# An S5 mixer on one core: states-to-outputs operand left compact, two products summed by TensorE

## The chip, the cores and the metric

The kernel runs on one core of a Trainium2 chip. The metric is the device time of one execution in microseconds (us). TensorE (PE in the profile; PEld is its weight load), VectorE (DVE), ScalarE (ACT), GpSimd (POOL) and SyncE (SP, which issues the transfers) each run a fixed order of instructions and wait for each other by semaphores.

## The reference

A trunk of two layers over 512 positions of 1024 features: an S5 state-space mixer, a shared key and value, a differential attention, a gated convolution MLP after each. Only the mixer is touched. Its core, with 64 groups of 16 channels and 64 complex states each:

```python
u = h @ w_in
def chunk_step(carry, u_chunk):
    x_r0, x_i0 = carry
    bu_r = jnp.einsum("tbgc,gpc->tbgp", u_chunk, bb_r)
    bu_i = jnp.einsum("tbgc,gpc->tbgp", u_chunk, bb_i)
    pw_r, pw_i, s_r, s_i = lax.associative_scan(_ssm_combine, (a_r, a_i, bu_r, bu_i), axis=0)
    x_r = s_r + pw_r * x_r0 - pw_i * x_i0
    x_i = s_i + pw_r * x_i0 + pw_i * x_r0
    y = (jnp.einsum("tbgp,gcp->tbgc", x_r, cr)
         - jnp.einsum("tbgp,gcp->tbgc", x_i, ci))
    return (x_r[-1], x_i[-1]), y
y = y + d_skip.astype(f32) * u.astype(f32)
g = jax.nn.gelu(y).astype(h.dtype)
val, gate = jnp.split(g @ w_glu, 2, axis=-1)
return val * jax.nn.sigmoid(gate)
```

## The kernel before

`ssm()` runs from about 26 to 168 us of the span. It treats the 64 groups in 8 blocks of 8 groups, as four pairs q of two groups g: the 128 partitions of a state tile hold the 64 states of both groups of a pair. Time is folded: four neighbouring positions make one of 128 columns, so that the positions inside a fold need a small Toeplitz product of their own.

For one block b the steps are, in the program's order:

- `cprod` (L479 to L494, VectorE): the compact tile `wo`, both operands of the block without the zeros; `ssm_coefs` loads its input `bc`.
- `ssm_prep` (L505): `pad` (L500, ScalarE) spreads `wo` into `wp` (states' inputs) and `op` (outputs). Each holds both groups of a pair side by side, zero where partition and column belong to different groups; a mask as the scale makes the zeros. `op` takes two calls of 128x512 for the four powers and two of 128x128 for slot 0, from `bc`. Then `wp` is turned (L522) and copied to `ctrl` (L523).
- `ssm_turn_u` (L552, L554): the inputs turned, `uc`. `ssm_toep` (L532): the Toeplitz operand from `wp` and `op`; it leaves PSUM by a ScalarE copy (L541) and a VectorE add of the skip term `dm` (L542), and is repeated down the partitions by three copies (L544).
- `ssm_inputs` (L563): the inputs of the states, `v`, to PSUM.
- `ssm_states` (VectorE): rotation by the tables `tab` (L582 into `za`, L583 into `zb`, added at L584), a scan for each of real and imaginary part (L586, from `za` into `zb`), rotation back: two products (L587 into `xs`, L588 into `za`) and their sum (L589, `xs` += `za`).
- `ssm_out`: `y` in one PSUM bank, for each pair q a Toeplitz product (L598) and two products with the states (L600, real and imaginary, all 128 partitions); then the gelu (L602). `ssm_turn`: `g` turned (L611, `gt`), split in a high and a low part (`hTh` L615 on ScalarE, `hTl` L616 on VectorE); `gv` is the product with `w_glu` that follows (L119 to L121, three passes: high by high, low by high, high by low), whose weights L103 (ScalarE) and L104 (VectorE) split as they come from HBM.

The loop `for b in range(-2, 11)` overlaps blocks: one turn holds `ssm_prep` and the inputs of block b+1, states and outputs of block b, the turn of b-1, the `gv` step of b-3 and the tables (`ssm_tables`, L460 to L474, with a GpSimd copy of `decay`, L467) of b+2. A scheduler fixes from it the order of each engine. The products of the second half of `u` (L119 to L121) fill in between. Two things tie the steps beside the data. The tag `tp` has two PSUM banks, shared in turn by `ct`, `ut`, `toep`, `gt` and `y`. The tags "xn" (`za`, `zb`) and "gain" (`xs`) have two buffers of 128x1024 each, so that a block's `za` and `zb` take the two of the block before.

Of the kernel before, what the change touches and what calls it, by code (L numbers as in the profile page):

```python
# [18 lines left out]
P = 128  # L19
# [33 lines left out]
class Trunk:  # L53
# [244 lines left out]
    def ssm_load(self, sp):  # L298
        nc, io = self.nc, self.io
        xk = io["x"].rearrange("t p d -> (t p) d").rearrange("(k j) d -> k j d", j=4)  # L300
        par = sp.tile([P, 158], F32, name="s5", bufs=1)
# [175 lines left out]
    def cprod(self, sp, m, b):  # L477


        V = self.nc.vector  # L480
        sh = [P, 8, 4, 16]
        wo = sp.tile([P, 2, 2, 4, 4, 16], F32, tag="wo", name=f"wo{b}", bufs=1)
        o = wo.rearrange("p r s q n c -> p r (s q) n c")
        t = sp.tile(sh, F32, tag="wot", name=f"wot{b}", bufs=1)
        k = [self.co[:, r, b].rearrange("p s q (n o) -> p (s q) n o", o=1).broadcast_to(sh) for r in range(2)]
        mr = [m[:, r].rearrange("p s q (o c) -> p (s q) o c", o=1).broadcast_to(sh) for r in range(2)]
        V.tensor_tensor(o[:, 0], k[0], mr[0], ALU.mult)
        V.tensor_tensor(t, k[1], mr[1], ALU.mult)
        V.tensor_tensor(o[:, 0], o[:, 0], t, ALU.subtract)
        t = sp.tile(sh, F32, tag="wot", name=f"wot2_{b}", bufs=1)  # L490
        V.tensor_tensor(o[:, 1], k[0], mr[1], ALU.mult)
        V.tensor_tensor(t, k[1], mr[0], ALU.mult)
        V.scalar_tensor_tensor(o[:, 1, :4], o[:, 1, :4], -1.0, t[:, :4], ALU.mult, ALU.subtract)
        V.tensor_tensor(o[:, 1, 4:], o[:, 1, 4:], t[:, 4:], ALU.add)  # L494
        return wo
    def pad(self, dst, src):

        for g in range(2):
            d = dst[:, :, :, g, :].rearrange("p (r q) n c -> p r q n c", r=2)
            self.nc.scalar.activation(d, src, AF.Copy, scale=self.maskS[:, g:g + 1])  # L500

    def ssm_coefs(self, sp, b):
        bc = sp.tile([P, 2, 2, 4, 16], F32, tag="bc", name=f"bc{b}", bufs=2)
        self.nc.sync.dma_start(bc, self.io["s5_bc"][b])
        return bc, self.cprod(sp, bc, b)  # L505

    def ssm_prep(self, sp, b, coefs):

        nc = self.nc
        bc, wo = coefs  # L510
        wp = sp.tile([P, 8, 4, 2, 16], F32, tag="wp", name=f"wp{b}", bufs=1)
        self.pad(wp, wo[:, :, 0])
        op = sp.tile([P, 8, 5, 2, 16], F32, tag="op", name=f"op{b}", bufs=2)
        self.pad(op[:, :, 1:], wo[:, :, 1])
        self.pad(op[:, :, 0:1], bc[:, :, 1].rearrange("p r q (o c) -> p r q o c", o=1))
        op = op.rearrange("p (r q) n g c -> p r q (n g c)", r=2)
        wp = wp.rearrange("p (r q) n g c -> p r q (n g c)", r=2)
# [6 lines left out]
        return ctrl, wp, op  # L524

    def ssm_toep(self, sp, b, wp, op):

        nc = self.nc
        ps = self.bank(f"toep{b}", "tp")
        for q in range(4):  # L530
            for r in range(2):
                nc.tensor.matmul(ps[:32, q * P:(q + 1) * P], wp[:, r, q, 0:32], op[:, r, q, 0:128],  # L532
                                 start=(r == 0), stop=(r == 1))
        toep = self.toep[b % 2]
        tv = toep.rearrange("p (q n) -> p q n", q=4)
        pv = ps.rearrange("p (q n) -> p q n", q=4)
        dm = sp.tile([32, 4, 32], F32, tag="dm", name=f"dm{b}", bufs=1)
        nc.gpsimd.tensor_tensor(dm, self.ident[:32, :32].rearrange("p (o c) -> p o c", o=1).broadcast_to([32, 4, 32]),
                                self.dskip[:32, 4 * b:4 * b + 4].rearrange("p (q o) -> p q o", o=1).broadcast_to([32, 4, 32]),
                                ALU.mult)  # L540
        nc.scalar.copy(tv[96:, :, 32:], pv[:32, :, 32:])  # L541
        nc.vector.tensor_tensor(tv[96:, :, :32], pv[:32, :, :32], dm, ALU.add)  # L542
        for j in range(1, 4):
            nc.scalar.copy(tv[96 - 32 * j:P - 32 * j, :, 32 * j:], tv[96:, :, :P - 32 * j])  # L544
        return toep

    def ssm_turn_u(self, sp, b, U):
# [18 lines left out]
    def ssm_states(self, sp, b, v, tab):  # L566

        nc, V = self.nc, self.nc.vector
        tab, dk = tab
        za = self.npool.tile([P, 2, 512], F32, tag="xn", name=f"za{b}")  # L570
        zb = self.npool.tile([P, 2, 512], F32, tag="xn", name=f"zb{b}")
        xs = self.npool.tile([P, 2, 512], F32, tag="gain", name=f"xs{b}")
        k4 = lambda z: z.rearrange("p r (q k) -> p r q k", q=4)
        new = lambda z: k4(z)[:, :, :, 1:]
        sh = [P, 2, 4, P - 1]
        both = lambda z, k: z.rearrange("p (r q k) -> p r q k", r=1, q=4)[:, :, :, k].broadcast_to(sh)

# [12 lines left out]
        return xs  # L590

    def ssm_out(self, sp, b, op, toep, uc, xs):
# [8 lines left out]
        g = sp.tile([P, 4, 4, 32], F32, tag="g", name=f"g{b}", bufs=2)  # L601
        nc.scalar.activation(g.rearrange("p i q e -> p q i e"), y.rearrange("p (q i e) -> p q i e", q=4, i=4),  # L602
                             AF.Gelu_apprx_tanh)
        return g
# [468 lines left out]
def pack(inp):  # L1073
# [21 lines left out]
    st = lambda n: a[n][0].reshape(32, 2, 64).transpose(1, 2, 0).reshape(P, 32)  # L1095
    grid = np.tile(np.concatenate([16 * np.arange(4), np.arange(16) + 0.5]).astype(np.float32), (P, 1))
    mask = (np.arange(P)[:, None] // 64 == np.arange(2)[None]).astype(np.float32)
    dsk = np.tile(a["ssm_d"][0].reshape(32, 32).T, (4, 1))
    cols = lambda g: g.reshape(KD, P).T
    dt = np.repeat(a["ssm_log_dt"][0].reshape(32, 2).T, 64, axis=0)  # L1100
    o["s5"] = np.concatenate([cols(a["ssm_norm"]), mask, dsk, st("ssm_lambda_re"), st("ssm_lambda_im"), grid, dt], 1)
# [45 lines left out]
```

## Time and profile before

| | us |
|---|---|
| median of 3 runs | 1348.28 |
| lowest, highest | 1346.69, 1348.58 |
| the profiled execution | 1347.01 |
| its span | 1345.2 |
| PE busy | 1313.6 (98%) |
| PEld busy | 1079.9 (80%) |
| DVE busy | 783.6 (58%) |
| ACT busy | 615.0 (46%) |
| POOL busy | 93.2 (7%) |

The span runs from the first to the last instruction of the profiled execution; its own time is 1.8 us longer. Busy shares are averages over stages with different limits, so the mixer is read by itself. The granted TensorE clock is given as a share of full speed (1.00 is 2.4 GHz, 0.50 is 1.2 GHz).

### The profile page before, as it was taken

What the parts mean: (1) busy time and instruction counts of PE and PEld (TensorE: products, weight loads), DVE (VectorE), ACT (ScalarE), POOL (GpSimd) and SP (SyncE); (2) the same over time, 40 slices, a digit from 0 to 9 for tenths busy, and PEclk for the clock granted to TensorE, in tenths of its full rate; (3) what the DMA queues carried; (4) which work ended last, traced back from release to release, by engine and by line L of the source; (5) the groups of instructions that cost most, each with busy time, mean ns of one, the idle gap of its engine ahead of it and who ended that gap; (6) DMA issues with size and microseconds to landing.
All of it is one profiled execution on the core that took longest, in us unless ns stands there. A gap on an engine that the chain in (4) does not pass through costs nothing.

```text
span 1345.2 us, 16605 instructions
## 1 busy us (share of the span) xinstructions
PE 1313.6 (98%) x6444; PEld 1079.9 (80%) x6444; DVE 783.6 (58%) x1314; ACT 615.0 (46%) x1049; POOL 93.2 (7%) x101
## 2 busy tenths in 40 slices
PE   7999799999999999999999999999999999999998
PEld 5787688988788888888887777688888888888887
DVE  8999834666633566444545665745766435664343
ACT  7899433544421344233535565644544323443242
POOL 2135000000000000000030121000000000000000
PEclk9999999999999999999999999999999999999999
DMA  6301422333333233323333102122333333333311
GB/s 219 106 25 44 134 94 63 106 104 95 95 96 101 85 95 104 102 79 106 114 111 125 62 2 73 53 69 75 125 94 94 110 95 91 99 101 100 95 56 39
DMA packets 37099, 122.31 MB, mean 91 GB/s; under 512 B 4339, under 2 KB 6387, under 8 KB 37020
## 3 DMA queue, kind: packets, MB, share of 16 engines
q1 hardware_dynamic: 35804, 119.07, 28.2%
q10 hardware_dynamic: 1184, 2.16, 0.4%
q8 instruction: 51, 0.84, 0.3%
q14 instruction: 28, 0.23, 0.1%
q0 software_dynamic: 32, 0.02, 0.0%
HBM read 119.12 MB, written 2.12 MB: 90 GB/s over the span
## 4 chain that ended last, share of the span: by engine, by line
PE 84%; DVE 11%; ACT 3%; issue 1%; DMA 0%; POOL 0%; SPq 0%; ACTq 0%; DVEq 0%
PE up L120 12%; PE up L119 12%; PE up L121 12%; PE dn L119 6%; PE dn L121 6%; PE dn L120 6%; PE pg L121 2%; PE pg L119 2%; PE pg L120 2%; PE s L957 2%; DVE zb L586 1%; PE o L979 1%; PE k L119 1%; PE q L119 1%; PE q L121 1%
## 5 line engine op out<-in xcount | busy, mean ns | idle before, releaser
L104 DVE TENSOR_TENSOR lo_wst<-wst,hi_wst 128x1024 fp32r<-128x1024 f32 x162 | 198.0, 1223 | 262.5 <-ACT hi_wst L103 262.0
L120 PE MATMUL up<-hTl,hi_wst 128*128 128x512 f32 (+1 forms) x768 | 285.6, 372 | 0.3 <-DVE hTl L167 0.3
L119 PE MATMUL up<-hTh,hi_wst 128*128 128x512 f32 (+1 forms) x768 | 285.1, 372 | 0.8 <-ACT hTh L166 0.7
L121 PE MATMUL up<-hTh,lo_wst 128*128 128x512 f32 (+1 forms) x768 | 285.1, 371 | 0.0
L103 ACT CAST hi_wst<-wst 128x1024 fp32r<-128x1024 f32 x162 | 169.8, 1049 | 231.5 <-PE dn L121 143.0
L119 PEld LDWEIGHTS up<-hTh,hi_wst 128*128 128x128 f32 x768 | 144.4, 188 | 26.8 <-ACT hTh L166 1.6
L120 PEld LDWEIGHTS up<-hTl,hi_wst 128*128 128x128 f32 x768 | 144.6, 188 | 25.6 <-DVE hTl L167 0.7
L121 PEld LDWEIGHTS up<-hTh,lo_wst 128*128 128x128 f32 x768 | 144.6, 188 | 24.9
L119 PE MATMUL dn<-hi_wst,ih 128*128 128x512 f32 x352 | 137.6, 391 | 0.0
L120 PE MATMUL dn<-lo_wst,ih 128*128 128x512 f32 x352 | 137.0, 389 | 0.0
L121 PE MATMUL dn<-hi_wst,il 128*128 128x512 f32 x352 | 136.4, 389 | 0.0
L243 DVE SCALAR_TENSOR_TENSOR acc<-up,cw,acc 128x511 f32<-128x511 f32 x88 | 65.7, 746 | 47.1 <-ACT acc L242 47.1
L242 ACT ACTIVATE acc<-up,cw 128x512 f32<-128x512 f32 x88 | 68.4, 777 | 47.3 <-PE up L121 47.3
L250 ACT CAST ih<-acc 128x512 fp32r<-128x512 f32 x44 | 27.3, 621 | 113.1 <-DVE acc L247 113.0
L119 PEld LDWEIGHTS dn<-hi_wst,ih 128*128 128x128 f32 x352 | 66.1, 188 | 14.5 <-issue 1.0
L109 DVE SCALAR_TENSOR_TENSOR lo_wst<-wst,gains,hi_wst 128x512 fp32r<-128x512 f32 x80 | 56.1, 746 | 37.0 <-ACT hi_wst L108 37.0
L121 PEld LDWEIGHTS dn<-hi_wst,il 128*128 128x128 f32 x352 | 66.1, 188 | 13.6
L120 PEld LDWEIGHTS dn<-lo_wst,ih 128*128 128x128 f32 x352 | 66.1, 188 | 13.5
L244 DVE SCALAR_TENSOR_TENSOR acc<-up,cw,acc 128x510 f32<-128x510 f32 x88 | 65.8, 748 | 2.9
L108 ACT ACTIVATE hi_wst<-wst,gains 128x512 fp32r<-128x512 f32 x80 | 53.4, 719 | 27.9 <-PE dn L121 16.9
L246 ACT ACTIVATE acc<-acc 128x512 f32<-128x512 f32 x44 | 27.8, 632 | 64.8 <-DVE acc L244 64.8
L121 PE MATMUL pg<-hi_wst,hTl 128*128 128x512 f32 (+1 forms) x128 | 49.2, 384 | 0.0
(267 smaller groups left out, 2221.7 us busy)
## 6 DMA issues: line engine op xcount, KB each, us to landing
wst<-in_w_up SPq DMA_DIRECT2D x88, 512.0 KB, 3.5
wst<-in_w_down SPq DMA_DIRECT2D x44, 512.0 KB, 3.6
wst<-in_w_glu SPq DMA_DIRECT2D x16, 512.0 KB, 3.6
wst<-in_w_gate SPq DMA_DIRECT2D x16, 512.0 KB, 3.6
wst<-in_kv_w SPq DMA_DIRECT2D x16, 512.0 KB, 4.5
wst<-in_w_in SPq DMA_DIRECT2D x8, 512.0 KB, 6.5
wst<-in_w_q SPq DMA_DIRECT2D x8, 512.0 KB, 4.7
wst<-in_w_o SPq DMA_DIRECT2D x8, 512.0 KB, 4.4
```

The source lines that it names most:

```text
L103: nc.scalar.copy(hi, st)
L104: nc.vector.tensor_tensor(lo, st, hi.bitcast(F32), ALU.subtract)
L108: nc.scalar.activation(hi[:, c], st[:, c], AF.Copy, scale=g[:, k:k + 1])
L109: nc.vector.scalar_tensor_tensor(lo[:, c], st[:, c], g[:, k:k + 1], hi[:, c].bitcast(F32), ALU.mult, ALU.subtract)
L119: nc.tensor.matmul(out, ah, bh, start=start, stop=False)
L120: nc.tensor.matmul(out, ah, bl, start=False, stop=False)
L121: nc.tensor.matmul(out, al, bh, start=False, stop=stop)
L242: nc.scalar.activation(c, ps[s], AF.Identity, bias=self.cw[:, n, 3:4], scale=self.cw[:, n, 2:3])
L243: nc.vector.scalar_tensor_tensor(c[:, 1:], ps[s][:, :T - 1], self.cw[:, n, 1:2], c[:, 1:], ALU.mult, ALU.add)
L244: nc.vector.scalar_tensor_tensor(c[:, 2:], ps[s][:, :T - 2], self.cw[:, n, 0:1], c[:, 2:], ALU.mult, ALU.add)
L246: nc.scalar.activation(acc[0], acc[0], AF.Gelu_apprx_tanh)
L250: nc.scalar.copy(ih, acc[1])
```

## The change

It does four things. (1) L589 goes: `xs` and `za` are both handed to TensorE, which multiplies each by the same operand and sums in PSUM. (2) `op` with its four ScalarE calls goes. The operand is `wo` itself, with a fifth slot, filled by a GpSimd copy (L496). Since it holds no zeros, each group's 64 states are multiplied alone, on half of TensorE's rows, into a PSUM bank of its own: 32 products of 64 rows and 64 columns a block instead of 8 of 128 by 128. The Toeplitz part of `y` becomes 8 products of 64 columns instead of 4 of 128. (3) The Toeplitz products (now L526) give 64 columns each instead of 128, and leave PSUM by two masked ScalarE calls (L535), with VectorE's add (L537) in SBUF behind them. (4) The gelu (L605) is two calls of 128x256. The other steps have new line numbers: `za`, `zb` and their sum L577, L578, L579; scan L581; back L582, L583; Toeplitz part and states part of `y` L594, L601; `v` L558; `gt` L614, `hTh` L618, `hTl` L619.

```diff
     def cprod(self, sp, m, b):
-        wo = sp.tile([P, 2, 2, 4, 4, 16], F32, tag="wo", name=f"wo{b}", bufs=1)
-        o = wo.rearrange("p r s q n c -> p r (s q) n c")
+        wo = sp.tile([P, 2, 2, 4, 5, 16], F32, tag="wo", name=f"wo{b}", bufs=3)
+        o = wo.rearrange("p r s q n c -> p r (s q) n c")[:, :, :, 1:, :]
...
+        self.nc.gpsimd.tensor_copy(wo[:, :, 1, :, 0, :], m[:, :, 1])
         return wo
...
-        self.pad(wp, wo[:, :, 0])
-        op = sp.tile([P, 8, 5, 2, 16], F32, tag="op", name=f"op{b}", bufs=2)
-        self.pad(op[:, :, 1:], wo[:, :, 1])
-        self.pad(op[:, :, 0:1], bc[:, :, 1].rearrange("p r q (o c) -> p r q o c", o=1))
+        for g in range(2):
+            nc.scalar.activation(wp[:, :, :, :, g, :], wo[:, :, 0, :, 1:, :], AF.Copy, scale=self.maskS[:, g:g + 1])
...
         for q in range(4):
             for r in range(2):
-                nc.tensor.matmul(ps[:32, q * P:(q + 1) * P], wp[:, r, q, 0:32], op[:, r, q, 0:128],
-                                 start=(r == 0), stop=(r == 1))
+                nc.tensor.matmul(ps[:32, q * 64:(q + 1) * 64], wp[:, r, q, 0:32],
+                                 wo[:, r, 1, q, :4, :].rearrange("p n c -> p (n c)"), start=(r == 0), stop=(r == 1))
...
-        nc.scalar.copy(tv[96:, :, 32:], pv[:32, :, 32:])
-        nc.vector.tensor_tensor(tv[96:, :, :32], pv[:32, :, :32], dm, ALU.add)
+        for g in range(2):
+            nc.scalar.activation(tv[96:, :, g, :], ps[:32, :256].rearrange("p (q n) -> p q n", q=4), AF.Copy,
+                                 scale=self.mask32[:, g:g + 1])
+        nc.vector.tensor_tensor(tv[96:, :, :, :16], tv[96:, :, :, :16], dm.rearrange("p q (g c) -> p q g c", g=2), ALU.add)
...
         V.tensor_tensor(new(za), both(zb[:, 1], now), pair(0, 1), ALU.mult)
-        V.tensor_tensor(xs, xs, za, ALU.add)
-        return xs
+        return xs, za
...
-        y = self.bank(f"y{b}", "tp")
+        y = [self.bank(f"y{b}_{g}", "tp") for g in range(2)]
+        at = lambda q: (slice(q * P, (q + 1) * P), slice(q * 64, (q + 1) * 64))
         for q in range(4):
-            c = slice(q * P, (q + 1) * P)
-            nc.tensor.matmul(y[:, c], uc[:, c], toep[:, c], start=True, stop=False)
-            for r in range(2):
-                nc.tensor.matmul(y[:, c], xs[:, r, c], op[:, r, q, 32:], start=False, stop=r == 1)
...
+            c, d = at(q)
+            for g in range(2):
+                nc.tensor.matmul(y[g][:, d], uc[:, c], toep[:, q * P + 64 * g:q * P + 64 * g + 64], start=q == 0, stop=False)
+        for q in range(4):
+            c, d = at(q)
+            for z in xs:
+                for r in range(2):
+                    for g in range(2):
+                        h = slice(64 * g, 64 * g + 64)
+                        nc.tensor.matmul(y[g][:, d], z[h, r, c], wo[h, r, 1, q, 1:, :].rearrange("p n c -> p (n c)"),
+                                         start=False, stop=q == 3 and r == 1 and z is xs[-1])
```

Between block 6's last product and block 7's states, VectorE's order before (the number behind a name is the block, the last one the tile's own; `wst` is a weight of `gv` or of the MLP):

```order
L588 TENSOR_TENSOR za6_1425<-zb6_1426,tab6_1249 128x8x127 [waits DVE_49]
L104 TENSOR_TENSOR lo_wst13_1626_1629<-wst13_1626,hi_wst13_1626_1628 128x1024 [waits DMAHW5_49]
L589 TENSOR_TENSOR xs6_1427<-xs6_1427,za6_1425 128x1024 [waits DVE_49]
L542 TENSOR_TENSOR toep1_296<-toep7_1446,dm7_1455 32x4x32 [waits Activation_49]
L616 TENSOR_TENSOR hTl_83<-gt5_1474,hTh_82 128x512 [waits Activation_49]
L582 TENSOR_TENSOR za7_1506<-v7_0_1481,tab7_1383 128x8x127 [waits PE_49]
L583 TENSOR_TENSOR zb7_1507<-v7_1_1482,tab7_1383 128x8x127 [waits DVE_49,PE_49]
L104 TENSOR_TENSOR lo_wst14_1632_1635<-wst14_1632,hi_wst14_1632_1634 128x1024 [waits DMAHW3_49]
L584 TENSOR_TENSOR za7_1506<-za7_1506,zb7_1507 128x1024 [waits DVE_49,Pool_49]
```

The same place with the change:

```order
L583 TENSOR_TENSOR za6_1574<-zb6_1575,tab6_1376 128x8x127 [waits DVE_49]
L104 TENSOR_TENSOR lo_wst15_1846_1849<-wst15_1846,hi_wst15_1846_1848 128x1024 [waits DMAHW4_49,Activation_49]
L537 TENSOR_TENSOR toep1_296<-toep1_296,dm7_1603 32x8x16 [waits Activation_49]
L619 TENSOR_TENSOR hTl_83<-gt5_1623,hTh_82 128x512 [waits Activation_49]
L577 TENSOR_TENSOR za7_1685<-v7_0_1630,tab7_1536 128x8x127 [waits DVE_49,PE_49]
L578 TENSOR_TENSOR zb7_1686<-v7_1_1631,tab7_1536 128x8x127 [waits PE_49]
L579 TENSOR_TENSOR za7_1685<-za7_1685,zb7_1686 128x1024 [waits DVE_49,Pool_49]
```

The add between the last product and the next block is gone. The product into `zb7` takes the buffer of `za6`; where the reader of `za6` was VectorE's own add, it is now TensorE's products into `y6`.

TensorE's order before around the outputs of block 5 (`v6` are the inputs of the states of block 6, `gt4` the turned outputs of block 4):

```order
L611 MATMUL gt4_1346<-ident_67,g4_1242 128x128 x3
L563 MATMUL v6_0_1353<-uc6_1310,ctrl6_1278 128x128 x4
L563 MATMUL v6_1_1354<-uc6_1310,ctrl6_1278 128x128 [waits DVE_49]
L563 MATMUL v6_1_1354<-uc6_1310,ctrl6_1278 128x128 x3
L119 MATMUL gv0_0_1062<-hi_wst10_1520_1522,hTh_82 128x512 [waits Activation_49]
L598 MATMUL y5_1363<-toep1_296,uc5_1182 128x128 [waits DVE_49]
L600 MATMUL y5_1363<-op5_1145,xs5_1293 128x128 [waits Pool_49]
L600 MATMUL y5_1363<-op5_1145,xs5_1293 128x128
```

And with the change:

```order
L614 MATMUL gt4_1469<-ident_67,g4_1368 128x128 x3
L558 MATMUL v6_0_1476<-uc6_1432,ctrl6_1401 128x128 x4
L558 MATMUL v6_1_1477<-uc6_1432,ctrl6_1401 128x128 [waits DVE_49]
L558 MATMUL v6_1_1477<-uc6_1432,ctrl6_1401 128x128 x3
L594 MATMUL y5_0_1486<-toep1_296,uc5_1278 128x64 [waits PE_49,Activation_49]
L594 MATMUL y5_0_1486<-toep1_296,uc5_1278 128x64 x3
L601 MATMUL y5_0_1486<-wo5_1233,xs5_1416 128x64 [waits DVE_49]
L601 MATMUL y5_0_1486<-wo5_1233,xs5_1416 128x64
L601 MATMUL y5_0_1486<-wo5_1233,za5_1414 128x64 [waits DVE_49,Pool_49]
L601 MATMUL y5_0_1486<-wo5_1233,za5_1414 128x64
L601 MATMUL y5_0_1486<-wo5_1233,xs5_1416 128x64 x2
L594 MATMUL y5_1_1487<-toep1_296,uc5_1278 128x64 [waits DVE_49]
```

The outputs of a block now fill two banks. The bank of the first half (`y5_0`) is that of the Toeplitz product; the second half (`y5_1`) takes the bank of `gt4`, which is free when `hTl` has been read from it, and waits for VectorE. Six products into the first half stand ahead of that wait by themselves; further down the two halves alternate.

## Rows read from the trace of the kernel before

**Rows 1.** The page's head.

```profile
span 1345.2 us, 16605 instructions
```

**Rows 2.** Busy time of each engine by windows of the mixer's loop, 42 to 166.1.

```profile
core 0: us, PE busy (x) PEld busy (x) DVE busy (x) ACT busy (x) POOL busy (x), PEclk, DMA share, GB/s
...
117.00:132.00 15.00, 13.41 (x93) 11.13 (x91) 14.94 (x20) 14.67 (x29) 7.73 (x6) 1.00 0.00 1
...
156.00:160.00 4.00, 0.00 (x0) 0.00 (x0) 4.00 (x5) 0.00 (x0) 0.00 (x0) 0.94 0.13 8
160.00:163.00 3.00, 2.94 (x14) 2.97 (x15) 1.05 (x1) 0.00 (x0) 0.00 (x0) 0.52 0.67 199
...
sum 124.10, PE 109.39 PEld 93.19 DVE 117.66 ACT 97.66 POOL 36.96; mean PE 9.94 PEld 8.47 DVE 10.70 ACT 8.88 POOL 3.36
```

**Rows 3.** Groups by line, DVE, 42 to 168: count | busy us, mean ns | idle before.

```profile
L104 DVE TENSOR_TENSOR lo_wst<-wst,hi_wst 128x1024 fp32r<-128x1024 f32 x9 | 10.9, 1213 | 0.0
...
L589 DVE TENSOR_TENSOR xs<-xs,za 128x1024 f32<-128x1024 f32 x8 | 9.7, 1214 | 0.0
...
L616 DVE TENSOR_TENSOR hTl<-gt,hTh 128x512 fp32r<-128x512 f32 x8 | 5.5, 685 | 5.2 <-ACT hTh L615 5.1
```

**Rows 4.** Chain in order of time, 113 to 160: start, us, what.

```profile
113.83 1.14 DVE xs L589
114.97 0.60 DVE wo L487
...
117.93 0.28 DVE toep L542
```

**Rows 5.** The loop's end in the timeline: start, us, what, [idle before <-releaser].

```profile
156.44 1.21 DVE L588 TENSOR_TENSOR za<-zb,tab 128x1016 f32<-128x1016 f32 x1
...
158.70 1.21 DVE L589 TENSOR_TENSOR xs<-xs,za 128x1024 f32<-128x1024 f32 x1
...
160.06 1.19 PE L600 MATMUL y<-op,xs 128*128 128x128 f32 x4 [4.46 <-DVE xs L589]
...
166.13 0.50 PE L119 MATMUL gv<-hi_wst,hTh 128*128 128x512 f32 x1 [0.67 <-ACT hTh L615]
```

**Rows 6.** Timeline of PE: one run of `v`, two neighbouring products of `gv`.

```profile
101.32 1.95 PE L563 MATMUL v<-uc,ctrl 128*128 128x128 f32 x16
...
152.69 0.39 PE L119 MATMUL gv<-hi_wst,hTh 128*128 128x512 f32 x1
...
152.92 0.40 PE L120 MATMUL gv<-lo_wst,hTh 128*128 128x512 f32 x1
```

**Rows 7.** Weight loads by line, PEld, 42 to 168.

```profile
L563 PEld LDWEIGHTS v<-uc,ctrl 128*128 128x128 f32 x128 | 14.9, 192 | 0.4 <-issue 0.2 <-ACT hi_wst L103 0.2
L532 PEld LDWEIGHTS toep<-op,wp 128*32 128x32 f32 x116 | 12.1, 110 | 1.2 <-ACT ctrl L523 1.2
...
L119 PEld LDWEIGHTS gv<-hi_wst,hTh 128*128 128x128 f32 x31 | 5.8, 188 | 1.9 <-ACT hTh L615 0.9
```

**Rows 8.** Weight loads of half the rows, attention scores, 700 to 900.

```profile
L957 PEld LDWEIGHTS s<-kT,qT 64*128 64x128 f32 x128 | 12.5, 184 | 9.4 <-issue 4.0 <-DVE mx L958 3.7 <-ACT qT L821 0.5
```

**Rows 9.** Timeline of PE: products on half the rows between products on all rows.

```profile
799.33 0.49 PE L957 MATMUL s<-kT,qT 64*128 64x128 f32 x4
799.75 0.33 PE L975 MATMUL pt<-ident,s 128*128 128x128 f32 x1
...
801.26 0.49 PE L957 MATMUL s<-kT,qT 64*128 64x128 f32 x2
801.67 0.33 PE L975 MATMUL pt<-ident,s 128*128 128x128 f32 x1
```

**Rows 10.** A GpSimd copy and the VectorE product at whose start it ends.

```profile
111.33 5.92 POOL L467 COPY decay<-sp 128x508 f32<-128x508 f32 x1 [4.84 <-DVE zb L586]
...
116.69 1.21 DVE L582 TENSOR_TENSOR za<-v,tab 128x1016 f32<-128x1016 f32 x1
```

**Rows 11.** A ScalarE pad that goes, by lines, 42 to 168.

```profile
L500 ACT ACTIVATE op<-wo,s 128x512 f32<-128x512 f32 x14 | 9.4, 713 | 0.0
```

More of the change, by code (lines that the diff above doesn't have):

```diff
@@ L300, in ssm_load @@
         xk = io["x"].rearrange("t p d -> (t p) d").rearrange("(k j) d -> k j d", j=4)
-        par = sp.tile([P, 158], F32, name="s5", bufs=1)
+        par = sp.tile([P, 160], F32, name="s5", bufs=1)
         self.arena = [self.npool.tile([P, D], F32, tag="gain", name=f"arena{n}") for n in range(2)]
@@ L313, in ssm_load @@
         self.gssm, self.maskS, self.dskip = par[:, :8], par[:, 8:10], par[:, 10:42]
-        self.lr, self.li, self.grid, self.log_dt = par[:, 42:74], par[:, 74:106], par[:, 106:126], par[:, 126:]
+        self.lr, self.li, self.grid, self.log_dt = par[:, 42:74], par[:, 74:106], par[:, 106:126], par[:, 126:158]
+        self.mask32 = par[:32, 158:]
         return st
@@ L494, in cprod @@
         V.tensor_tensor(o[:, 1, 4:], o[:, 1, 4:], t[:, 4:], ALU.add)
+        self.nc.gpsimd.tensor_copy(wo[:, :, 1, :, 0, :], m[:, :, 1])
         return wo
[L496 to L500, printed above, removed]
     def ssm_coefs(self, sp, b):
@@ L504, in ssm_coefs, with ssm_prep @@
         self.nc.sync.dma_start(bc, self.io["s5_bc"][b])
-        return bc, self.cprod(sp, bc, b)
-    def ssm_prep(self, sp, b, coefs):
+        return self.cprod(sp, bc, b)
+    def ssm_prep(self, sp, b, wo):
         nc = self.nc
-        bc, wo = coefs
-        wp = sp.tile([P, 8, 4, 2, 16], F32, tag="wp", name=f"wp{b}", bufs=1)
-        self.pad(wp, wo[:, :, 0])
-        op = sp.tile([P, 8, 5, 2, 16], F32, tag="op", name=f"op{b}", bufs=2)
-        self.pad(op[:, :, 1:], wo[:, :, 1])
-        self.pad(op[:, :, 0:1], bc[:, :, 1].rearrange("p r q (o c) -> p r q o c", o=1))
-        op = op.rearrange("p (r q) n g c -> p r q (n g c)", r=2)
-        wp = wp.rearrange("p (r q) n g c -> p r q (n g c)", r=2)
+        wp = sp.tile([P, 2, 4, 4, 2, 16], F32, tag="wp", name=f"wp{b}", bufs=1)
+        for g in range(2):
+            nc.scalar.activation(wp[:, :, :, :, g, :], wo[:, :, 0, :, 1:, :], AF.Copy, scale=self.maskS[:, g:g + 1])
+        wp = wp.rearrange("p r q n g c -> p r q (n g c)")
         ctrl = sp.tile([P, 2, 512], F32, tag="ctrl", name=f"ctrl{b}", bufs=2)
@@ L523, in ssm_prep, with ssm_toep @@
             nc.scalar.copy(ctrl[:, r, :], ps)
-        return ctrl, wp, op
-    def ssm_toep(self, sp, b, wp, op):
+        return ctrl, wp, wo
+    def ssm_toep(self, sp, b, wp, wo):
         nc = self.nc
@@ L531, in ssm_toep @@
             for r in range(2):
-                nc.tensor.matmul(ps[:32, q * P:(q + 1) * P], wp[:, r, q, 0:32], op[:, r, q, 0:128],
-                                 start=(r == 0), stop=(r == 1))
+                nc.tensor.matmul(ps[:32, q * 64:(q + 1) * 64], wp[:, r, q, 0:32],
+                                 wo[:, r, 1, q, :4, :].rearrange("p n c -> p (n c)"), start=(r == 0), stop=(r == 1))
         toep = self.toep[b % 2]
[L535 to L539, printed above, removed]
+        tv = toep.rearrange("p (q g n) -> p q g n", q=4, g=2)
+        dm = sp.tile([P, 4, 32], F32, tag="dm", name=f"dm{b}", bufs=1)[96:]
+        nc.gpsimd.tensor_tensor(dm, self.ident[96:, 96:].rearrange("p (o c) -> p o c", o=1).broadcast_to([32, 4, 32]),
+                                self.dskip[96:, 4 * b:4 * b + 4].rearrange("p (q o) -> p q o", o=1).broadcast_to([32, 4, 32]),
                                 ALU.mult)
-        nc.scalar.copy(tv[96:, :, 32:], pv[:32, :, 32:])
-        nc.vector.tensor_tensor(tv[96:, :, :32], pv[:32, :, :32], dm, ALU.add)
+        for g in range(2):
+            nc.scalar.activation(tv[96:, :, g, :], ps[:32, :256].rearrange("p (q n) -> p q n", q=4), AF.Copy,
+                                 scale=self.mask32[:, g:g + 1])
+        nc.vector.tensor_tensor(tv[96:, :, :, :16], tv[96:, :, :, :16], dm.rearrange("p q (g c) -> p q g c", g=2), ALU.add)
         for j in range(1, 4):
-            nc.scalar.copy(tv[96 - 32 * j:P - 32 * j, :, 32 * j:], tv[96:, :, :P - 32 * j])
+            nc.scalar.copy(tv[96 - 32 * j:P - 32 * j, :, :, 16 * j:], tv[96:, :, :, :64 - 16 * j])
         return toep
@@ L588, in ssm_states, with ssm_out @@
         V.tensor_tensor(new(za), both(zb[:, 1], now), pair(0, 1), ALU.mult)
-        V.tensor_tensor(xs, xs, za, ALU.add)
-        return xs
-    def ssm_out(self, sp, b, op, toep, uc, xs):
+        return xs, za
+    def ssm_out(self, sp, b, wo, toep, uc, xs):
         nc = self.nc
-        y = self.bank(f"y{b}", "tp")
+        y = [self.bank(f"y{b}_{g}", "tp") for g in range(2)]
+        at = lambda q: (slice(q * P, (q + 1) * P), slice(q * 64, (q + 1) * 64))
         for q in range(4):
-            c = slice(q * P, (q + 1) * P)
-            nc.tensor.matmul(y[:, c], uc[:, c], toep[:, c], start=True, stop=False)
-            for r in range(2):
-                nc.tensor.matmul(y[:, c], xs[:, r, c], op[:, r, q, 32:], start=False, stop=r == 1)
[L601 to L604, printed above, removed]
+            c, d = at(q)
[9 more added lines that the diff above has]
+                                         start=False, stop=q == 3 and r == 1 and z is xs[-1])
+        out = sp.tile([P, 4, 4, 32], F32, tag="g", name=f"g{b}", bufs=2)
+        for g in range(2):
+            nc.scalar.activation(out[:, :, :, 16 * g:16 * g + 16].rearrange("p i q c -> p q i c"),
+                                 y[g][:, :256].rearrange("p (q i c) -> p q i c", q=4, i=4), AF.Gelu_apprx_tanh)
+        return out
     def ssm_turn(self, b, g):
@@ L1097, in pack @@
     mask = (np.arange(P)[:, None] // 64 == np.arange(2)[None]).astype(np.float32)
+    mask32 = (np.arange(P)[:, None] // 16 % 2 == np.arange(2)[None]).astype(np.float32)
     dsk = np.tile(a["ssm_d"][0].reshape(32, 32).T, (4, 1))
@@ L1100, in pack @@
     dt = np.repeat(a["ssm_log_dt"][0].reshape(32, 2).T, 64, axis=0)
-    o["s5"] = np.concatenate([cols(a["ssm_norm"]), mask, dsk, st("ssm_lambda_re"), st("ssm_lambda_im"), grid, dt], 1)
+    o["s5"] = np.concatenate([cols(a["ssm_norm"]), mask, dsk, st("ssm_lambda_re"), st("ssm_lambda_im"), grid, dt, mask32], 1)
     bm = lambda n: a[n][0].reshape(32, 2, 64, 16).transpose(1, 2, 0, 3).reshape(P, 8, 4, 16)
```

## Prediction

> **What bounds the kernel now.** I read the page's head first [rows 1]: a span of 1345.2 us. The edits touch only the mixer's loop, and what follows it is the same work in the same order, so a microsecond won or lost in the loop's end is a microsecond of the kernel. The windows of the loop [rows 2] are the next view. VectorE is busy 117.66 of 124.10 us, and 14.94 of the 15 from 117 to 132, TensorE 13.41 there; over the whole loop TensorE has 109.39. VectorE's idle time is 6.4 us, of which 5.1 lie at the end, where hTl waits for hTh [rows 3]. So VectorE sets the pace with at most 1.4 us to spare, and TensorE is second, not far behind. At the loop's end [rows 5] the chain leaves VectorE: the last product L588 starts at 156.44, a weight split and L589 follow, TensorE idles from 156 to 160, starts y at 160.06 and gv at 166.13; from 160 to 163 its granted clock is 0.52, half of 2.4 GHz, after that idle time [rows 2].
>
> **VectorE's part.** L589 goes. The chain gives it 1.14 us from start to start [rows 4]; seven of the eight lie ahead of the last L588: -8.0. The order puts one more weight split (L104, about the same size [rows 3]) ahead of that point, +1.1, and one hTl less, -0.6 by the spacing of 128x512 operations [rows 4]. With the idle 1.4 the most that this side gives is -8.9.
>
> Against it stands a new wait. The product L578 into zb of block b+1 overwrites za of block b, which TensorE now reads until y of b is done. Behind L578 on VectorE are the sum, the scans and all that follows, so the wait delays everything. Between the end of L583 and L578 VectorE has only other work as cover. For block 6 that is, by the order: L104 1.14, the Toeplitz add 0.28, hTl 0.60 and L577 1.13 [rows 4, 5], together 3.15 us. TensorE needs longer: the second half of y takes the bank that hTl frees, 2.0 us in, then four Toeplitz products (8 passes) and 16 pairs of states products (32 passes) at 0.11 us: 2.0 + 0.9 + 3.6 = 6.5 us. The wait is about 3.5. Worked out alike, with the work that the order puts between as cover, blocks 0 to 6 have 4.0, 6.1, 10.9, 7.4, 5.9, 4.5 and 3.2 us of cover, and waits of 0, 0, 0.6, 4.4 (TensorE is late there with other products), 0, 1.3 and 3.5: 9.8 us. VectorE's account ends at -8.9 + 9.8, about **+1**. At the loop's end L589 and a split (2.3 us) and the half clock go, but y has twice the products and waits for hTl of block 6: from the end of L588 to gv it was 8.5 us, and I make the same again.
>
> **TensorE's part.** An fp32 product has two passes. One pass costs 0.112 us: 16 passes of v take 1.95 [rows 6], less a tail of 0.16 (a gv product shows 0.39 while the next starts 0.23 later [rows 6]). The loop has 436 such passes (128 of v, 116 recorded of the Toeplitz products [rows 7], 192 of y), 116 turning ones that I price alike, and 186 products of u and gv at 0.23 (six groups of 31 [rows 7]): 48.6 + 12.8 + 42.8 = 104.2 us of 124.1, idle 19.9.
>
> - The Toeplitz products have 64 columns instead of 128. The nearest row is their own: loads of 32 columns take 110 ns against 192 of v's 128 [rows 7], so a shorter load shows and the stream is next to bind. I take half a pass off for each of 128: -7.1. Bounds: 0 and -7.1.
> - y's Toeplitz part has 64 more passes, which load the same 128 columns: +7.1; bounds 0 (if 64 columns halve the pass) and +7.1.
> - y's states part: 256 products of half the rows in place of 64. Among the attention scores two halves' products (four passes) delay the next turning product by 0.42 us, one half's (two passes) by 0.41 [rows 9]: two halves run beside each other, and a switch to or from half rows costs about 0.2. The order lets 220 products alternate, and leaves 36 alone in blocks 3, 5 and 7, where the second half waits for its bank. That is (110 + 36) x 2 = 292 passes of 0.112, 32.6 us, against 128 passes, 14.3: +18.3. Bounds: +2 if a pass of 64 columns takes half, +43 if the halves run one after the other.
> - About 15 switches of 0.2: +3.
>
> The sum is 104.2 + 21.3 = 125.5 us. To it come 2.6 us in which TensorE must idle: about 2.0 from the end of y to gv, for gelu, turn and hTh [rows 5], and 0.6 for hTl before the last y. That is 128.1 where the loop has 124.1: **+4**. TensorE, with less than 20 us to spare, is asked for 21, and takes VectorE's place as the limit. VectorE's account of +1 is not added to it: its new waits are TensorE's lateness seen from the other side.
>
> A rule of the Trainium skill speaks against the change here: "TensorE: Matmul & The Clock Gate", section on LDWEIGHTS, says that a weight load goes by its columns and not by the rows it fills. The trace agrees: loads of 64 rows take 184 ns [rows 8], those of 128 rows 192 [rows 7]. By that rule alone, with each half paying a full load, the states part would be the +43 above. The Trainium skill's "TensorEngine Tiling (Array Packing)", section Key Properties, says that tiles load and multiply in parallel and that a change of tiling drains the array, and the trace agrees (0.42 for two, 0.41 for one [rows 9]).
>
> **The smaller parts.** ScalarE loses four pads a block, two of 713 ns [rows 11], and gains one call each in the Toeplitz evacuation and the gelu. It is not the limit (97.66 of 124.10 [rows 2]): 0; if VectorE waits for it in the first blocks, -0.9. GpSimd's copy into slot 0 stands ahead of nothing on its engine that is short of time except the memsets of the states; beside VectorE such a copy can stretch to 5.92 us, but it ended 0.56 us into a product that reads PSUM, L582 [rows 10], and the new copy has the same chance: 0, bound +4.5. The Toeplitz add leaves PSUM for SBUF at the same size: 0.
>
> **The rivals.**
>
> *VectorE's saving stays.* If a half-row pass of 64 columns takes less than a full one (the bounds +2 and +18 are far apart, and the scores' products [rows 9], too few in a row, cannot tell), TensorE's addition falls. At 0.08 us a pass y's pairs need 2.6 us, which leaves block 6 a wait of 2.4 and block 3 a shorter one; the waits fall to 3 to 4, and VectorE's account decides: -8.9 + 3.5, about -5, that is 1343. It decides once TensorE's additions are under about 14 us. For it: VectorE bounds the loop now, and the add is certain to go. Against it: loads of 64 rows are as long as those of 128 [rows 8].
>
> *The halves do not overlap in a long run.* The trace shows pairs of two halves only [rows 9]. If 32 in a row run one after the other, the states part is 512 passes, +43 instead of +18: TensorE is short by 25 more, 1348 + 4 + 20, about 1372 (part of it under what now idles). The half-row form would then not do what it is for.
>
> *The narrow products keep the pace of the wide ones.* If the Toeplitz products of 64 columns still take a whole pass, -7.1 becomes 0: +11, 1359.
>
> **How the numbers follow.** The sum is made against the profiled execution, 1.3 us under the median of the runs; added to the median of 1348.28 it gives 1348.3 + 4 = **1352**. Chances: TensorE becomes the limit at 0 to +8, 0.44; VectorE's saving stays, -2 to -7, 0.36; narrow products, 0.10; no overlap, 0.10. About 0.2% (2.7 us) can be told from no change. Faster takes the most of the second case, 0.30; no change the rest of it and the lower part of the first, 0.22; slower what is left, 0.48. The range reaches from the second case's middle, 1342, to just over the third, 1362; below and above lie about 0.1 each. The likeliest case's own range is 1348 to 1356.
>
> **What would show it.** Right: VectorE idle before L578, released by y, 8 to 10 us in all with the longest at blocks 3 and 6; VectorE's share from 57 to 147 under 95%; TensorE with hardly any gaps there; y's states part at about 3.6 us a block; the Toeplitz products at half their time; the granted clock 1.00 at the loop's end. Wrong: y in under 3 us, VectorE still full and the last gv group ahead of 166.1 (the first rival); L601's passes one by one at 0.11 (the second); L526 no shorter (the third); or VectorE waiting for GpSimd's copy.

## The result and the profile after

| | before | with the change |
|---|---|---|
| median, 6 runs each (us) | 1348.36 | 1366.97 |
| lowest to highest | 1346.4 to 1351.47 | 1361.84 to 1371.11 |
| the profiled execution | 1347.01 | 1369.45 |
| its span, mean granted clock | 1345.2, 0.998 | 1367.7, 0.987 |

The ratio is 1.0141, with an interval of 1.0123 to 1.0158: the change makes the kernel slower by 1.4%, 18.6 us. The forecast was 1352, with 1342 to 1362 as the range. The direction held; the size was five times what was forecast, and outside the range.

The page of the changed kernel, its span, its busy times, and TensorE's granted clock in 40 slices of 34 us:

```profile
span 1367.7 us, 17517 instructions
...
PE 1351.3 (99%) x6892; PEld 1116.8 (82%) x6892; DVE 776.9 (57%) x1306; ACT 606.0 (44%) x1033; POOL 82.0 (6%) x109
...
PEclk9998889999999999999999999999999999999999
```

All of the loss is in the mixer: the last `gv` product ends at 235.3 us instead of 212.7, and what follows takes 1132 us in both kernels. There the clock's row shows something that the kernel before had only for a few us at the loop's end [rows 2]. In windows of 2 us around the outputs of block 5 (busy time of PE, PEld, DVE, ACT, POOL, then the granted clock, DMA share, GB/s):

```profile
142.00:144.00 2.00, 2.00 (x17) 1.86 (x17) 2.00 (x3) 1.81 (x5) 0.00 (x0) 1.00 0.00 0
144.00:146.00 2.00, 2.00 (x24) 2.00 (x24) 0.87 (x3) 1.42 (x2) 0.00 (x0) 0.61 0.00 0
146.00:148.00 2.00, 2.00 (x23) 2.00 (x22) 0.00 (x0) 0.58 (x1) 0.00 (x0) 0.50 0.00 0
...
152.00:154.00 2.00, 2.00 (x7) 1.52 (x6) 2.00 (x2) 0.00 (x0) 0.00 (x0) 0.50 0.00 0
154.00:156.00 2.00, 2.00 (x13) 1.75 (x12) 2.00 (x3) 1.39 (x2) 0.00 (x0) 0.83 0.00 0
156.00:158.00 2.00, 2.00 (x24) 1.53 (x23) 1.49 (x2) 1.31 (x4) 0.12 (x1) 1.00 0.03 10
```

TensorE falls from 2.4 to 1.2 GHz in the window from 144 and is back in the one from 154, while the profile shows it busy all the time. The same happens from 110 to 122 and from 174 to 190, and nowhere else up to the span's end: inside or just behind the outputs of blocks 3, 5 and 7, the three in which 12 to 16 products stand alone, without one of the other half beside them. (In block 4 four stand alone, and the clock stays.) In the timeline of PE (start, us, what), block 4's alternating products, two gv products at full clock, then block 5 as its clock falls, and gv after it:

```profile
129.01 0.27 PE L601 MATMUL y<-wo,xs 64*128 64x64 f32 x1
129.07 0.27 PE L601 MATMUL y<-wo,za 64*128 64x64 f32 x1
...
133.22 0.39 PE L121 MATMUL gv<-hi_wst,hTl 128*128 128x512 f32 x1
133.45 0.39 PE L119 MATMUL gv<-hi_wst,hTh 128*128 128x512 f32 x1
...
143.19 0.66 PE L601 MATMUL y<-wo,xs 64*128 64x64 f32 x4
143.68 0.61 PE L601 MATMUL y<-wo,za 64*128 64x64 f32 x4
...
144.90 0.42 PE L601 MATMUL y<-wo,za 64*128 64x64 f32 x1
145.00 0.42 PE L601 MATMUL y<-wo,xs 64*128 64x64 f32 x1
...
150.53 0.63 PE L119 MATMUL gv<-hi_wst,hTh 128*128 128x512 f32 x1
150.96 0.63 PE L120 MATMUL gv<-lo_wst,hTh 128*128 128x512 f32 x1
```

At full clock the passes of alternating halves start 0.06 us apart, two per 0.112: they overlap, as [rows 9] had it. The lone ones start 0.11 to 0.12 apart (the four passes at 143.19 take 0.49 us to the next start). After the fall the alternating ones are 0.10 to 0.11 apart and gv 0.43 instead of 0.23. By lines, 42 to 192 (the first number is busy us, then the mean ns, then the idle time before it):

```profile
L578 DVE TENSOR_TENSOR zb<-v,tab 128x1016 f32<-128x1016 f32 x8 | 9.7, 1213 | 15.3 <-PE y L601 15.3
...
L526 PE MATMUL toep<-wo,wp 128*32 128x64 f32 x112 | 7.5, 220 | 0.1
```

VectorE's new wait for y is there, 15.3 us in all, and the Toeplitz products of 64 columns are short.

**The half clock's price.** T us of busy TensorE at half clock do the work of T/2, and lower the mean clock of the span by T/2 over the span. So (1 - mean clock) x span is what a run lost, to about 0.7 us by the rounding of the clock. The six runs of the change have clocks of 0.993, 0.990, 0.990, 0.987, 0.987 and 0.986 for 1361.84, 1364.21, 1364.76, 1369.19, 1369.45 and 1371.11 us. Less their loss they come to 1350.6 to 1352.3, so that of 9 us of difference the clock leaves less than 2. For the 22 runs of the kernel before beside a later experiment the same gives 1343.2 to 1347.9, with losses of 1 to 5 us. These do not come together as well, probably because TensorE is not the limit there and a part of the half clock costs nothing.

### The profile page after: what moved, and what is told of

Its sections match the earlier page's. It is cut to its first block, busy times and chain, and to the rows that moved or that the text cites. A ratio compares the mean times of both kernels' runs of the same rounds, so it can differ in the third digit from the quotient of the medians.

```text
span 1367.7 us, 17517 instructions
## 1 busy us (share of the span) xinstructions
PE 1351.3 (99%) x6892; PEld 1116.8 (82%) x6892; DVE 776.9 (57%) x1306; ACT 606.0 (44%) x1033; POOL 82.0 (6%) x109
## 4 chain that ended last, share of the span: by engine, by line
PE 90%; DVE 6%; ACT 2%; issue 1%; DMA 0%; POOL 0%; SPq 0%; ACTq 0%; DVEq 0%
PE up L120 12%; PE up L119 12%; PE up L121 12%; PE dn L119 6%; PE dn L121 6%; PE dn L120 6%; PE y L601 3%; PE pg L120 2%; PE pg L119 2%; PE pg L121 2%; PE s L960 2%; PE o L982 1%; PE gv L119 1%; PE gv L121 1%; PE gv L120 1%; PE k L119 1%
```

## The experiments

Three theories: A, the clock; B, the added passes cost what they cost whatever the clock does; C, VectorE's wait for y. All times below are medians beside runs of the kernel before on the same chip; "at full clock" means less the loss as above.

### 1. Halves alternating in every block (pair)

```diff
         for q in range(4):
             c, d = at(q)
             for g in range(2):
-                nc.tensor.matmul(y[g][:, d], uc[:, c], toep[:, q * P + 64 * g:q * P + 64 * g + 64], start=q == 0, stop=False)
+                last = nc.tensor.matmul(y[g][:, d], uc[:, c], toep[:, q * P + 64 * g:q * P + 64 * g + 64], start=q == 0, stop=False)
+        with self.tc.issue_after(last.ins):
...
```

All states products stand behind the second half's Toeplitz products, so the halves alternate in all eight blocks.

> Theory A (clock): TensorE's half clock after the lone half-row products of blocks 3, 5 and 7 costs about 17 us, so with the two halves alternating in every block the granted clock stays 1.00 from 42 to 190, and the time is 1349 to 1356. Theory B (work): the added passes cost the 19 us whatever the clock does, so the time stays at 1362 to 1371. Theory C (wait): VectorE's wait for y before the next block's second product is the cost; it is longer here, since the states products wait for the second bank, so 1368 or more.

Measured: 1355.0 (ratio 1.0043, 1.0024 to 1.0062), 12 us less than the change. The clock is 0.994 to 1.000; at full clock the eight runs give 1347.8 to 1349.2. The two with the clock at 0.999 and 1.000 took 1350.18 and 1349.23. C is refuted: VectorE waits about as long as before.

```profile
DVE zb L578 <- PE y L602: 13.3, 5, 3.8
```

A holds for most of the loss, but not wholly: most runs still had falls, fewer and shorter (the profiled one from 88 to 99 and from 128 to 136, not at the same blocks). Both of these came inside alternating products, a few us behind a short idle time of TensorE (0.7 us in the window from 84, 0.5 in those from 124 and 126).

### 2. All of one half ahead of the other (apart)

```diff
-        for q in range(4):
-            c, d = at(q)
-            for z in xs:
-                for r in range(2):
-                    for g in range(2):
-                        h = slice(64 * g, 64 * g + 64)
+        for g in range(2):
+            h = slice(64 * g, 64 * g + 64)
+            with self.tc.issue_after(last.ins):
+                for q in range(4):
+                    c, d = at(q)
+                    for z in xs:
+                        for r in range(2):
...
```

> The change with all products of the first half ahead of all of the second, in every block. Theory A: the halves no longer overlap (512 passes of 0.11 instead of 292, 24 us more) and the clock falls behind the outputs of nearly every block, 5 us lost each time; over 1400. Theory B: 24 us more, 1388 to 1395, with no more time at half clock than the change has.

Measured: 1411.07 (1.0446 to 1.049), the clock 0.968 to 0.972, at full clock 1368.6 to 1370.0. The loss is 39 to 45 us. In the profile the clock falls in each of the eight blocks, every time inside the lone products, with no idle time of TensorE just before. Here are those of a block that start at 76.0:

```profile
76.00:78.00 2.00, 2.00 (x19) 2.00 (x18) 2.00 (x4) 1.98 (x5) 0.00 (x0) 1.00 0.19 20
78.00:80.00 2.00, 2.00 (x12) 2.00 (x12) 1.79 (x2) 1.06 (x1) 0.00 (x0) 0.55 0.79 250
80.00:82.00 2.00, 2.00 (x15) 2.00 (x15) 0.00 (x0) 0.78 (x2) 0.00 (x0) 0.50 0.61 211
```

A as expected; B, with no more half clock than the change, is refuted.

### 3. The same passes on all rows (full_narrow)

Is it half of the rows, or many narrow products in a row? This run takes the padded operand of the kernel before, hands the sum to TensorE and cuts each states product into two of 64 columns: 64 passes a block, one after the other, as in experiment 2, but on 128 rows. (zb stands in the other buffers, as in experiments 5 and 6.)

```diff
-            for r in range(2):
-                nc.tensor.matmul(y[:, c], xs[:, r, c], op[:, r, q, 32:], start=False, stop=r == 1)
+            for z in xs:
+                for r in range(2):
+                    for h in range(2):
+                        d = slice(q * P + 64 * h, q * P + 64 * h + 64)
+                        nc.tensor.matmul(y[:, d], z[:, r, c], op[:, r, q, 32 + 64 * h:96 + 64 * h],
+                                         start=False, stop=r == 1 and h == 1 and z is xs[-1])
```

> sum_full_buf with each states product cut into two of 64 columns: as many products, passes and columns a block as the halves apart have (64 passes, one after the other), but on all 128 rows with the padded operand. If half rows by themselves bring the clock down, it stays at 0.998 or more here and the time is that of TensorE's work alone, 1365 to 1375. If narrow products in a row do it, whatever the rows, the clock falls as with the halves apart (0.97) and the time is 1400 or more. If a pass of 64 columns is shorter than 0.11 us on all rows, it is under 1360.

Measured: 1370.67 (1.016 to 1.0194), within 2 us of experiment 2 at full clock, and the clock 1.000 in all four runs. From 42 to 222:

```profile
42.00:222.00 180.00, 179.47 (x1254) 162.10 (x1253) 125.11 (x150) 110.30 (x199) 15.84 (x33) 1.00 0.20 65
```

and the same window with the halves apart:

```profile
42.00:222.00 180.00, 178.22 (x1157) 161.59 (x1156) 111.13 (x134) 93.70 (x171) 15.99 (x38) 0.81 0.18 53
```

TensorE is busy for 179 and 178 of 180 us; the one keeps its clock, the other has 0.81. The same number of passes of the same width in y's states part costs 40 us more on half the rows, nearly all of it by the clock. Narrow products in a row are not the cause by themselves.

The two runs differ in more than the rows: in full_narrow half of the operand is zeros, the Toeplitz products have 128 columns, `y` has one bank, and `zb` other buffers. The Toeplitz products and the banks are the same in experiments 1 and 2, and the clock is 0.994 to 1.000 in the one and 0.968 to 0.972 in the other by the order of the half-row products alone; the buffers did not keep the clock in experiment 5 (0.984 to 0.986). What the zeros do was not tested.

### 4. Wide products in between (mid_buf, add_mid, apart_mid)

Was it that TensorE goes too long without wide products? Half of a block's 12 wide gv products (all of a u step in the first three blocks) move into the middle of y's states products.

```diff
-                    gv.step(b - 3)
+                    gv.step(b - 3, (0, 1) if on(b) else None)
...
+                    wide = (lambda: gv.step(b - 3, (2, 3))) if on(b - 3) else (lambda: u1.step(U1[b][0]))
-                    gs[b] = self.ssm_out(sp, b, prep[b][2], toep[b], uc[b], xs[b])
+                    gs[b] = self.ssm_out(sp, b, prep[b][2], toep[b], uc[b], xs[b], wide)
...
+                if hq:
+                    wide()
```

> pair_buf with half of the 12 wide gv products of a block (u in the first three) moved into the middle of y's states products. If the clock falls where TensorE has gone for several us through narrow fp32 products alone, it stays at 1.00 in every run, and none comes to 1352; two more switches a block cost about 3 us: 1348 to 1351. If the half-row products themselves bring it down, some runs still show 0.996 and 1352.

> add_pair with the same wide products in the middle of y. add_pair had 0.995 to 0.999, up to 7 us at half clock. If the stretch of narrow products is the cause, the clock is as in the kernel before or higher, and the time 1340 to 1343 with the switches; if the half-row products are, it stays 1343 to 1348.

> The run with the halves apart (1411, clock 0.969 to 0.972, 1369 without the loss), with the same wide products between the halves. If the stretch of narrow products is the cause, most of the falls go: 1370 to 1380, clock 0.99 or more. If the lone half-row products are the cause, the falls stay: 1400 to 1415.

Measured: 1356.89 (1.0061 to 1.0091; clock 1.000, 1.000, 0.997, 0.995), 1352.59 (1.0029 to 1.0058; 0.993 to 0.995) and 1427.7 (1.0578 to 1.0633; 0.964 to 0.969). The mean clock stays under 1.000 in two of four runs, in all five and in all four, and the halves apart lose even 44 to 52 us. The times are longer than either alternative gave: at full clock the medians are 5 to 13 us above those of the same runs without the interruption.

Only the halves apart can answer the question. The profiled run of mid_buf has no fall in the mixer, and both falls of add_mid's (at 53.6 and 162.9) follow idle time of TensorE, busy 0.58 us in the window from 52 and 0.05 in the one from 158. In apart_mid the clock falls fifteen times in the mixer, all but once without idle time just before, and in most blocks twice. In one of them the first half's products end at 81.8 at half clock; the clock comes back during the twelve wide products of u that follow, and falls again at 90.2, in the second half's products, which start at 87.06:

```profile
86.00:88.00 2.00, 2.00 (x12) 1.41 (x11) 0.00 (x0) 0.63 (x1) 0.00 (x0) 0.79 0.02 8
88.00:90.00 2.00, 2.00 (x20) 2.00 (x20) 0.00 (x0) 0.00 (x0) 0.00 (x0) 1.00 0.00 0
90.00:92.00 2.00, 2.00 (x10) 1.79 (x10) 0.68 (x1) 0.68 (x2) 0.51 (x3) 0.56 0.04 8
```

So the sixteen lone half-row products of one half, right behind wide ones, are enough; a long stretch without wide products is not needed.

### 5. VectorE's wait taken away (buf, pair_buf)

`zb` goes from the tag "xn" to "gain", where `xs` is. Then the next block's `za` and `zb` take buffers that TensorE is done with, and only L582 can still wait for y.

```diff
-        zb = self.npool.tile([P, 2, 512], F32, tag="xn", name=f"zb{b}")
+        zb = self.npool.tile([P, 2, 512], F32, tag="gain", name=f"zb{b}")
```

> The change with zb in the other pair of buffers, so that VectorE's second product of the next block no longer waits for y. The order now lets more products of one half run alone (in blocks 1, 5, 6 and 7). Theory A (clock): the wait was little of the loss, the lone products bring the half clock back, 1358 to 1372. Theory C (wait): the loss goes with the wait, 1341 to 1350.

> As buf, but with the halves alternating in every block. Theory A: VectorE's wait gone and the clock falling as seldom as in pair or less; what is left is TensorE's added work of about 21 us against 20 of idle time: 1346 to 1353. Theory C: as the run with the alternating halves and the wait differ by the wait alone, 13 us of it would come off 1355: 1341 to 1344.

Measured for the change with this edit: 1375.43 (1.019 to 1.0221), slower still and over the range of both theories. The order now lets some 85 products run alone, where the trace of the change shows about 44; the clock is 0.984 to 0.986, and at full clock it takes 1354.1 to 1355.5, 3 us more than the change. Some forty more lone products, each pair of which takes 0.22 us more, would be 4 to 5 us. The wait did not go altogether: L582 waits 8.7 us for y.

With the halves alternating no wait of VectorE for y is left among its longer ones, and the time is 1348.24 (0.9999 to 1.0021), no change against the kernel before; seven of ten runs have the clock at 0.999 or 1.000 and take 1347.6 to 1348.5, the others 0.996 and 1352 to 1353. The median at full clock is 1347.5, where experiment 1 has 1348.8. So 13 us of wait were worth about 1 us at full clock: TensorE was the limit, and VectorE's wait its shadow. C falls for the second time. The medians as measured differ by 7 us, because fewer runs lost the clock (three of ten, where it was six of eight); whether the wait had a part in that was not tested.

### 6. The two parts of the change, each alone (sum_full, sum_full_buf, add_kept, add_pair)

The add left to TensorE, on all rows with the padded operand, without and with zb's other buffer:

```diff
-        V.tensor_tensor(xs, xs, za, ALU.add)
-        return xs
+        return xs, za
...
-            for r in range(2):
-                nc.tensor.matmul(y[:, c], xs[:, r, c], op[:, r, q, 32:], start=False, stop=r == 1)
+            for z in xs:
+                for r in range(2):
+                    nc.tensor.matmul(y[:, c], z[:, r, c], op[:, r, q, 32:], start=False, stop=r == 1 and z is xs[-1])
```

> The kernel before with only the add left to TensorE: padded operand, 16 products of all 128 rows and 128 columns a block instead of 8. Theory A: no lone half-row products, no fall of the clock but at the loop's end; TensorE gets 14 us more and has 20 idle, VectorE saves up to 9 less its new waits; 1341 to 1349. Theory B: two thirds of the 19 us, 1358 to 1363. Theory C: the wait for y is there as in the change; with y at 3.6 us it is the same length, 1362 or more.

> The kernel before with the add left to TensorE on all rows, and zb in the other pair of buffers. TensorE has 14 us more and 20 idle, the half clock is as in the kernel before. If the new wait of VectorE is what held the run without this edit at 1353, it comes to 1340 to 1346; if TensorE's added work did, it stays at 1351 to 1355.

Measured: 1353.37 (1.0026 to 1.0052), between what the theories gave (A had 1341 to 1349), and with the buffer 1348.25 (0.9994 to 1.0013). The clock is 0.998 or more in both. Here the wait did cost something, 5 us:

```profile
DVE zb L583 <- PE y L600: 8.7, 4, 3.0
```

Without it the sum on TensorE, 14 us of added passes in 20 of idle time against 9 us saved on VectorE, comes out at no change. That lies between the two ranges expected, 1340 to 1346 and 1351 to 1355. A likely reason is that idle time of an engine that others wait for is not all to be had; no run shows it.

The compact operand alone, VectorE's add kept, in the scheduler's order and with the halves alternating:

```diff
-        return xs, za
+        V.tensor_tensor(xs, xs, za, ALU.add)
+        return (xs,)
```

> VectorE's add is back and each half has 16 products a block instead of 32. Theory A: fewer lone half-row products in a row, so the clock falls less often or not at all; TensorE's addition is about 5 us instead of 21 and hides in its idle time; 1346 to 1352. Theory B: about half of the 19 us remains, 1356 to 1360. Theory C: the wait is gone (nobody but VectorE reads za), 1346 to 1350.

> VectorE's add kept, halves alternating in every block: the compact operand alone, with no lone half-row products. Theory A: the run without the alternation lost 6.8 us at half clock in its profile (the kernel before 1.7); without these it comes to 1342 to 1346. Theory B: half rows cost their work, which did not change: 1347 to 1350.

(The first expectation counts passes: each half has 8 products of two passes a block instead of 16.)

Measured: 1348.18 (0.9992 to 1.0016) with the clock at 0.992 to 0.996, and 1343.54 with the halves alternating, **0.9965 (0.9954 to 0.9977)**, which beats both kernels. At full clock the two are at 1339.9 to 1342.0 and 1339.0 to 1342.5. The first lost 5 to 11 us by the clock, and the alternation got most of that back. The first lies in the ranges of A and of C, the second in A's.

Not all of these losses come from half-row products. Of the three falls in the first run's profile, those at 69 and 151 come inside or just behind them with TensorE busy, and the one at 123.5 behind idle time. One of the seven runs of the second still lost 7 us (clock 0.995, 1347.81); it is the profiled one, and both of its falls follow idle time, as the loop's end of the kernel before has it [rows 2]. The first of them:

```profile
118.00:120.00 2.00, 1.14 (x22) 1.00 (x18) 2.00 (x4) 1.97 (x4) 0.34 (x2) 1.00 0.00 0
120.00:122.00 2.00, 0.58 (x3) 0.58 (x4) 2.00 (x3) 1.37 (x3) 0.00 (x0) 0.80 0.00 0
122.00:124.00 2.00, 2.00 (x10) 1.82 (x9) 2.00 (x3) 1.16 (x3) 0.00 (x0) 0.50 0.65 150
```

| | median | mean clock | at full clock |
|---|---|---|---|
| the change | 1366.97 | 0.986 to 0.993 | 1350.6 to 1352.3 |
| halves alternating | 1355.0 | 0.994 to 1.000 | 1347.8 to 1349.2 |
| halves apart | 1411.07 | 0.968 to 0.972 | 1368.6 to 1370.0 |
| as many passes on all rows | 1370.67 | 1.000 | 1370.5 to 1371.5 |
| sum by TensorE alone, on all rows, with the buffer | 1348.25 | 0.999 to 1.000 | 1346.2 to 1349.3 |
| compact operand alone, alternating | 1343.54 | 0.995 to 0.999 | 1339.0 to 1342.5 |

## Why the prediction was wrong

- **What was right.** TensorE becomes the limit and VectorE is no longer full: from 102 to 117 it is busy 7.21 us of 15, where the kernel before shows 14.94 of 15 from 117 to 132 [rows 2].

```profile
102.00:117.00 15.00, 15.00 (x112) 14.07 (x111) 7.21 (x12) 9.72 (x20) 0.91 (x4) 0.78 0.28 80
```

- **TensorE's sum.** The change at full clock is at 1350.6 to 1352.3, and the sum gave 1352. A part of that is luck: the kernel before is at 1343 to 1348 at full clock, so that the added work is nearer 6 us than 4. The terms that can be read: two alternating passes took 0.112 us, as forecast, and lone passes 0.11 to 0.12, as forecast. The passes of y's Toeplitz part kept their length (eight in 0.93 us at 139.74), as forecast. The Toeplitz products of 64 columns do take half a pass less: sixteen end within 1.08 us where they took 1.94, 0.86 saved a block and 6.9 us in all, where 7.1 was the term.
- **The step that failed.** "TensorE with hardly any gaps" was taken to mean full clock: the forecast listed "the granted clock 1.00 at the loop's end" among the signs of being right, and priced every pass from 42 to 166 at full clock. The loss of clock was a term put at nothing. The one fall that the loop of the kernel before showed followed 4 us of idle time [rows 2], and I took idle time for the only cause. What the runs showed instead: a TensorE that the profile shows busy, on half of its rows without the other half beside it, loses the clock too. It cost the change 10 to 19 us a run; the miss against 1352 is 15.
- **The lone products.** I had counted 36 lone products, 0.112 us a pass; the trace shows about 44, four of them in block 4 and sixteen in block 7. They were the right thing to look at, with the wrong price: they take the clock from what follows, 5 to 7 us a fall in the profiled run.
- **VectorE's wait** was forecast at 9.8 us and is 15.3; how much of the excess is TensorE at half clock was not separated. That it is TensorE's lateness seen from the other side was right: taking 13 us of it away gained 1 us at full clock (experiment 5).
- **The rivals.** The halves overlap, so the second rival is refuted although its 1372 lies nearest to the time: the right size from the wrong mechanism. The third, narrow products that keep the pace of wide ones, is refuted for the Toeplitz products, where the weights have 32 columns, and true of `y`'s Toeplitz part, where they have 128. The first, VectorE's saving staying, needed half-row passes cheaper than 0.112 us a pair, and they were not. No engine is seen to wait for GpSimd's copy.
- The Trainium skill's "TensorE: Matmul & The Clock Gate", Part 1, ties the clock to how busy TensorE has been. The trace agrees for the falls behind idle time (the kernel before: 0.00 us busy from 156 to 160, clock 0.52 from 160 to 163 [rows 2]). For the others, by the busy share that the profile shows, it does not: the clock fell in windows where TensorE was busy 2.00 of 2.00 us, and the measurement decides.

## What to carry to other kernels

Look at the granted clock by stretches before anything else when a TensorE change misses its forecast, and take (1 - mean clock) x span off each run: if runs that scatter come together, it is the clock. Then look at what TensorE did before each fall: idle time and lone half-row products both showed up here, and a mean does not tell them apart. Products on half of the rows are cheap only as long as both halves alternate in the order that the engine really has; a bank that comes late can make them run alone, so hold the early half back until both can go. And do not count on all of the idle time of the second fullest engine when you move work to it: 14 us of work in 20 us of idle time gained nothing here.

## What the runs showed of the hardware that I had not expected

- TensorE's clock fell from 2.4 to 1.2 GHz while the profile shows it busy, inside or just behind runs of fp32 products on 64 of 128 rows: in blocks 3, 5 and 7 of the change, in all eight blocks with the halves apart (0.97 over the span). It kept 1.000 with the same number of passes of 64 columns on all rows.
- The clock also fell behind idle time of TensorE, and on all rows too: in the windows from 118 and 120, where add_pair's falls, it is busy 1.14 and 0.58 of 2.00 us, and in those from 84 and 86, where sum_full's falls, 1.33 and 0.76.
- Two halves that alternate, 16 products of each a block, lose it less often, but still in some runs (0.996 in three of ten of pair_buf, 0.994 to 0.996 in six of eight of pair). The three such falls in the two profiles come inside alternating products with 0.4 to 0.7 us of idle time shortly before; which of the two matters, and why one run falls and the next does not, stays open.
- On all rows a pass of 64 columns with 128 columns of weights takes as long as one of 128 columns: eight in 0.90 us (95.44 to 96.34), 0.112 each, as those of v [rows 6].

```profile
95.44 1.06 PE L602 MATMUL y<-op,za 128*128 128x64 f32 x8
96.34 0.44 PE L597 MATMUL y<-toep,uc 128*128 128x128 f32 x2
```

Not tried: a half-row form in which both halves have their banks from the start.
